# The seams of the two MLPs rebuilt: output projection in groups of 2 and 6 tiles, another order of the up tiles and of the operand loads, and the page sums moved

## The chip, the cores and the metric

One core of a Trainium2 chip runs the whole program. The metric is the device time of one execution in microseconds (us), lower is better. The kernel before takes 2758.23 us, the median of three runs (2755.21 to 2761.97). The names of the engines are those of the profile: PE is TensorE with its weight loads as PEld, DVE is VectorE, ACT is ScalarE, POOL is GpSimd, and SP is SyncE, which here issues nearly all DMAs.

## The reference

One step of a decoder with two layers, on 1088 tokens (1024 of a prompt and 64 of eight samples), model width 1024, hidden width 4096. Layer 0 mixes with a diagonal state-space model (S5) and a gated unit (GLU), layer 1 with a forgetting attention over a paged cache; each also attends to a small memory, and each ends with an output projection, an RMS norm and a squared-ReLU MLP:

```
def rmsnorm(x, g):
    y = x32 * lax.rsqrt(jnp.mean(x32 * x32, axis=-1, keepdims=True) + RMS_EPS)
    return (y * g.astype(jnp.float32)).astype(x.dtype)

def sqrelu_mlp(x, w_up, w_down):
    h = jax.nn.relu(x @ w_up)
    return (h * h) @ w_down
```

The attention of layer 1 also needs, per head, running sums of the log-forget values of the cached rows (the page sums): they are gathered through the page table, summed along the past, and the total is subtracted.

## The kernel before

Activations stand with the model width on the partitions and the tokens along the free dimension. The tokens form four chunks of 272 columns (`CH`); two chunks together are a half (`g`), so the two halves hold chunks 0 and 1, and 2 and 3.

Every fp32 operand is split into a high part, rounded by ACT, and a low part, the rest, subtracted by DVE (`split`, L213, L220 and L221); three matmuls then make one product (`mm3`). The big products of the MLP go through a scheme with seven sub-products instead of eight (`seven`, L390): an operand matrix of 2 by 2 blocks is turned into seven combinations (`operands`, L340, for the activations, with the subtractions L350, L351, L354 and L357; `weight_ops`, L363, for the weights, with four additions on POOL, L379 to L385), and all seven are split.

The stretch this document is about runs once in each layer:

1. The mixer ends. In layer 0 that is the GLU, with the attention to memory (`mem_attn`, L596) beside it. Then POOL issues 16 indirect DMAs that gather the page rows (L1220).
2. The output projection (`out_proj`, L316, over `dense`, L239) has eight weight tiles of 128 columns in two groups of four. For each group the four chunks are gone through in order, each tile of a chunk being 24 matmuls, and DVE adds the result to the residual (L323). Between the groups the page sums are worked out on DVE in layer 0 (L1225 to L1229).
3. With the second group of tiles a chunk is complete and `mlp_norm` (L419) starts: squares on ACT (L257), their sums on DVE (L259, L260), a matmul with ones for the sum over partitions, the scale (L271 to L274), eight multiplications of DVE by the scale and the gain (L432), and then the operands of the up projection; all that needs one chunk alone for chunks 0 and 2, and what combines both chunks of a half for chunks 1 and 3.
4. The up projection (`mlp`, L448) runs over 16 weight tiles `j`, each of 168 matmuls in seven products (12 matmuls for one product and one half), with the first tile done half by half. Its results are squared (L487 to L489), made into the seven operands of the down projection (`to_hidden`, L460), and stored in DRAM as `hops` (operand i, block b = j // 2); those of tiles 14 and 15 are stored plainly as `hcnv`.
5. The down projection (L524) runs over blocks 0 to 6 of the hidden width with seven operands each, loaded from `hops` by SP in pieces of 1088 KB (L514) into eleven places taken in turn (`hplace`), and block 7 is done plainly from `hcnv`. Each block is four passes of seven products of 12 matmuls.

The program is written in text order and then reordered, engine by engine, by a scheduler that simulates a timeline; buffers are rings and carved phases, and whoever writes a buffer waits for its last readers. Each engine then goes through its own list in order, SP's list of DMA issues too.

## Time and profile before

| what | value |
|---|---|
| median of 3 runs | 2758.23 us (2755.21 to 2761.97) |
| the profiled execution | 2760.94 us, of which its span on the core 2759.2 us |
| PE busy | 2575.1 us, 93% of the span, 20345 matmuls |
| DVE busy | 2023.4 us, 73% |
| POOL busy, ACT busy | 1249.9 us and 1239.9 us, 45% each |
| DMA | 561.64 MB, 204 GB/s over the span |
| mean granted clock of PE | 0.97 |

Busy time is the time in which an engine has an instruction in work. A stretch in which PE is less than fully busy is read with the count of matmuls in it: the same number at the pace of a full stretch would need less time, and the difference is what the stretch loses. Places in the trace are given in microseconds from the start of the span; layer 0's output projection begins near 405 and layer 1's near 1932.

### The profile page before, as it was taken

Reading aid. Unit: us, or ns where it says so; the run is one execution under the profiler, and the core shown is the slowest. Engines: PE = TensorE matmul, PEld = TensorE weight load, DVE = VectorE, ACT = ScalarE, POOL = GpSimd, SP = SyncE. Lnnn points to the kernel's source line nnn. Section 1 sums busy time; section 2 is a strip of 40 time slices with the busy share of each in tenths; the row PEclk is TensorE's granted clock in tenths of the full one; section 3 lists DMA queues with packets and bytes.
Section 4 is the critical chain, followed back from the end, with each engine's and each line's share of the span. In section 5 each row is a group of like instructions: output and inputs, shape, how many; then the busy total and the mean of one; then the engine's idle time right before and its main releaser. Section 6 shows DMA issues by size and latency. Waiting matters only on the chain.

```text
span 2759.2 us, 54020 instructions
## 1 busy us (share of the span) xinstructions
PE 2575.1 (93%) x20345; PEld 2404.4 (87%) x20345; DVE 2023.4 (73%) x3421; ACT 1239.9 (45%) x2544; POOL 1249.9 (45%) x1142
## 2 busy tenths in 40 slices
PE   5887898799998999999999999999879999899998
PEld 5877798799997999999889867777879999799997
DVE  8898655999985777784323278885499999577776
ACT  5433542566663222244322377773256666422224
POOL 4577411332231699842311455551033233169984
PEclk8999899899998999999999999999989999999999
DMA  6445332265668566543476899984226556866741
GB/s 200 109 110 165 105 122 83 82 248 229 234 241 314 208 258 266 198 157 108 147 261 218 265 303 312 305 296 159 96 88 249 230 236 238 306 238 242 280 170 65
DMA packets 242282, 561.64 MB, mean 204 GB/s; under 512 B 54053, under 2 KB 129382, under 8 KB 224614
## 3 DMA queue, kind: packets, MB, share of 16 engines
q1 hardware_dynamic: 212646, 548.50, 55.5%
q10 hardware_dynamic: 28864, 8.92, 1.4%
q8 instruction: 160, 2.62, 0.4%
q0 software_dynamic: 512, 0.79, 0.1%
q14 instruction: 100, 0.82, 0.1%
HBM read 386.19 MB, written 171.93 MB: 202 GB/s over the span
## 4 chain that ended last, share of the span: by engine, by line
PE 56%; DVE 18%; POOL 9%; DMA 8%; issue 4%; ACT 4%; another core or an unknown queue 1%; SPq 0%; POOLq 0%; ACTq 0%; DVEq 0%
PE banks L208 54%; DVE rounded L221 5%; POOL plain L539 4%; DMA hops<-plain 2%; DVE plain L221 2%; DMA rounded<-hops 2%; PE banks L1558 1%; POOL plain L547 1%; ACT rounded L220 1%; POOL plain L381 1%; POOL plain L379 1%; POOL plain L380 1%; ACT plain L220 1%; POOL plain L385 1%
## 5 line engine op out<-in xcount | busy, mean ns | idle before, releaser
L208 PE MATMUL banks<-rounded 128*128 128x272 f32 (+4 forms) x11552 | 1626.2, 296 | 97.6 <-ACT rounded L220 27.7
L208 PEld LDWEIGHTS banks<-rounded 128*128 128x128 f32 x11552 | 1521.3, 192 | 148.4 <-issue 32.2
L220 ACT ACTIVATE rounded<-plain 128x512 fp32r<-128x512 f32 (+5 forms) x575 | 384.3, 679 | 641.5 <-PE banks L208 473.2
L221 DVE TENSOR_TENSOR rounded<-plain,rounded 128x512 fp32r<-128x512 f32 (+4 forms) x520 | 490.8, 954 | 107.4 <-ACT rounded L220 103.3
L208 PE MATMUL banks<-mlp,rounded 128*128 128x272 f32 x3840 | 526.2, 292 | 18.0 <-DVE plain L536 5.4
L208 PEld LDWEIGHTS banks<-mlp,rounded 128*128 128x128 f32 x3840 | 502.1, 191 | 24.2 <-DVE rounded L221 8.0
L379 POOL TENSOR_TENSOR plain<-plain 128x512 f32<-128x512 f32 x60 | 98.5, 1642 | 709.2 <-DVE rounded L221 709.2
L539 POOL TENSOR_TENSOR plain<-plain,flex 128x544 f32<-128x544 f32 x192 | 292.0, 1531 | 42.0 <-DVE plain L538 39.3
L221 DVE TENSOR_TENSOR plain<-plain 128x544 fp32r<-128x544 f32 x212 | 209.8, 1006 | 28.0 <-ACT plain L220 21.9
L220 ACT ACTIVATE plain<-plain 128x544 fp32r<-128x544 f32 x212 | 136.6, 653 | 187.9 <-DMA hops<-plain 103.6
L538 DVE TENSOR_TENSOR plain<-banks,plain 128x544 f32<-128x544 f32 x192 | 137.7, 718 | 57.7 <-PE banks L208 54.9
L385 POOL TENSOR_TENSOR plain<-plain 128x512 f32<-128x512 f32 x60 | 101.1, 1685 | 65.6 <-DVE rounded L221 65.0
L208 PE MATMUL banks<-layer 128*32 128x256 f32 (+3 forms) x1152 | 110.7, 368 | 5.4 <-ACT layer L1381 2.1
L208 PE MATMUL banks<-flexr,rounded 128*128 128x272 f32 x768 | 107.4, 288 | 1.9 <-DVE flexr L221 1.9
L221 POOL TENSOR_TENSOR rounded<-plain,rounded 64x512 fp32r<-64x512 f32 (+2 forms) x55 | 77.4, 1414 | 67.4 <-ACT rounded L220 61.9
L221 POOL TENSOR_TENSOR rounded<-flex,rounded 128x544 fp32r<-128x544 f32 (+7 forms) x100 | 66.7, 675 | 87.7 <-ACT rounded L220 75.0
L208 PEld LDWEIGHTS banks<-flexr,rounded 128*128 128x128 f32 x768 | 100.6, 188 | 2.3 <-DVE flexr L221 2.3
L381 POOL TENSOR_TENSOR plain<-plain 128x512 f32<-128x512 f32 x60 | 101.1, 1685 | 3.0
L220 ACT ACTIVATE rounded<-banks 128x512 fp32r<-128x512 f32 (+2 forms) x136 | 75.0, 559 | 51.8 <-PE banks L1558 28.8
L221 DVE TENSOR_TENSOR rounded<-banks,rounded 128x512 fp32r<-128x512 f32 (+2 forms) x136 | 86.0, 637 | 15.1 <-ACT rounded L220 13.2
L487 DVE TENSOR_TENSOR plain<-banks,plain 128x544 f32<-128x544 f32 (+1 forms) x136 | 92.6, 681 | 4.7 <-PE banks L208 4.4
L380 POOL TENSOR_TENSOR plain<-plain 128x512 f32<-128x512 f32 x60 | 93.2, 1553 | 4.7
(359 smaller groups left out, 3135.2 us busy)
## 6 DMA issues: line engine op xcount, KB each, us to landing
hops<-plain SPq DMA_DIRECT2D x196, 544.0 KB
rounded<-hops SPq DMA_DIRECT2D x66, 1088.0 KB
plain<-in_cache_kT SPq DMA_DIRECT2D x128, 384.0 KB
layer<-in_cache_v SPq DMA_DIRECT2D x128, 384.0 KB
mlp<-hops SPq DMA_DIRECT2D x32, 1088.0 KB
plain<-in_w_up SPq DMA_DIRECT2D x32, 1024.0 KB
plain<-in_w_down SPq DMA_DIRECT2D x28, 1024.0 KB
plain<-in_xT SPq DMA_DIRECT2D x8, 1088.0 KB
```

The source lines that it names most:

```text
L208: PE.matmul(out, a, b, start=first, stop=last)
L220: S.activation(H, src, AF.Copy)
L221: e.tensor_tensor(L, src, H.bitcast(F32), op=ALU.subtract)
L379: G.tensor_tensor(a22, a21, a22, op=ALU.add)
L380: G.tensor_tensor(a21, a11, a21, op=ALU.subtract)
L381: G.tensor_tensor(a11, a22, a11, op=ALU.subtract)
L385: G.tensor_tensor(a12, a12, a11, op=ALU.subtract)
L487: V.tensor_tensor(x, ps, u, op=ALU.add)
L538: V.tensor_tensor(h, ps, h, op=ALU.add)
L539: G.tensor_tensor(h, h, u, op=ALU.add)
L547: G.tensor_tensor(hc, hc, hr[:, m, :], op=ALU.add)
L1558: PE.transpose(tb[:, k, 128 * i:128 * i + 128], p[i][:, 2 * c + k, :], ident)
```

## The change

It has five parts.

- **Output projection.** The groups are now 2 tiles and 6 tiles. The split weights of tiles 6 and 7 lie in two of the four `Pq` places of the MLP. The step between the groups is gone.
- **Norm.** Except for the last chunk, the sums of squares are made by POOL, and the eight multiplications of DVE become one multiplication by the scale over 128x2176 elements on DVE and eight multiplications by the gain on ACT; the low parts of operands 2 and 6 are split by POOL. Operand 6 of the first half is put off until the norm of the last chunk.
- **Up tiles.** The order is 14, 0, 1, ..., 13, 15, and tile 14's weights have their low parts split by POOL.
- **Up to down.** The weights and all seven operand loads of block 0 are asked for behind the products of tile 15 and ahead of that tile's own stores; the places and their order are new, the loads are issued in a chain, each behind the one before, and the load of the residual stands behind the operands of its block.
- **Page sums.** The 16 indirect DMAs and the sums stand in the text of the GLU loop (before chunk 1 and before chunk 3) and use raw weight buffers (`wf[2:4]`). The scheduler puts the DMAs ahead of that, among POOL's last S5 units.

The core of the diff:

```diff
-    def out_proj(ys, w, hs, done, between=None):
-        for g in range(2):
-            if g and between:
-                between()
-
+    def out_proj(ys, w, hs, done):
+
+        Pq[:] = phase_mlp()
+        more = [Pq[i].sub(WT * j, WT).at([128, 8, 128], F32R) for i in (2, 3) for j in range(2)]
...
+        for g, n in ((0, 2), (2, 6)):
...
-            dense([w[4 * g + i] for i in range(4)], ys, ev, done=(lambda c: done(hs[c], c)) if g else None)
+            dense([(m, w[m]) for m in range(g, g + n)], ys, ev, load, done=(lambda c: done(hs[c], c)) if g else None)
...
         w = CH[c][1]
-        s1 = rms_sums(h, w)
+        last = c == NC - 1
+        s1 = rms_sums(h, w, V if last else G)
         SY.dma_start(out=hmid[c], in_=h)
...
         def rest():
             rs = rms_scale(s1, w)
-            for k in range(8):
-                V.scalar_tensor_tensor(x[:, k, :], h[:, k, :], gains[:, gi, k:k + 1], rs,
-                                       op0=ALU.mult, op1=ALU.mult)
+            if last:
+                for k in range(8):
+                    V.scalar_tensor_tensor(x[:, k, :], h[:, k, :], gains[:, gi, k:k + 1], rs,
+                                           op0=ALU.mult, op1=ALU.mult)
+            else:
+                V.tensor_tensor(x, h, rs[:, None, :].broadcast_to([128, 8, w]), op=ALU.mult)
+                for k in range(8):
+                    S.mul(x[:, k, :], x[:, k, :], gains[:, gi, k:k + 1])
...
+                    split(o[:, 0], o[:, 1], t, G if i in (2, 6) and not last else V)
...
+            if c % 2 == 0:
+                operands(*b, extra, put_of(g), (0, 2))
+            elif not last:
+                operands(*b, extra, put_of(g), (1,))
+                held.append(lambda: operands(*b, extra, put_of(g), (6,)))
+            else:
+                held.pop()()
+                operands(*b, extra, put_of(g), (1, 6))
...
+        hplace = [setB[2], setB[3], setB[0], setC[2], setB[1], *Pq, setC[3], setC[1]]
...
+        def load_on(to, src):
+            with after(loads[-1]) if loads else nullcontext():
+                loads.append(SY.dma_start(out=to, in_=src))
+
+        def next_operands(b):
+
+            t = [hring([128, 2, 2, 2 * CN], F32R) for _ in range(7)]
+            r = [t[i] for i in (0, 5, 1, 6, 2, 3, 4)] if b == 0 else t
+            for i in range(7):
+                load_on(r[i].bitcast(F32), hops[i][b])
+            return r
...
+        jorder = (14, *range(14), 15)
+        W = up_weights(14, G)
+        for n, j in enumerate(jorder):
...
             if j < 15:
-                W = up_weights(j + 1)
-            to_hidden(j, q, tmps(sh))
+                W = up_weights(jorder[n + 1])
+            else:
+                W = down_weights(0, 0)
+                ops = next_operands(0)
+            to_hidden(j, q)
...
+        if c == 1:
+            past_rows()
+        if c == 3:
+            past_sums()
```

Where instructions move, at three places. First SP's list at the step from up to down of layer 0. `hops0` to `hops6` are the stored operands, `rounded`, `mlp1` to `mlp3` the places that they are loaded into, `hcnv` the plain stores of the last tiles. Before:

```order
L514 DMA mlp1_4125<-hops6_76 128x2176
L514 DMA rounded_65<-hops1_71 128x2176
L514 DMA mlp2_4126<-hops0_70 128x2176
L514 DMA rounded_65<-hops2_72 128x2176
L514 DMA mlp3_4127<-hops1_71 128x2176
L514 DMA rounded_65<-hops3_73 128x2176
L477 DMA hcnv_77<-plain_64 128x2x272
L514 DMA rounded_65<-hops4_74 128x2176
L477 DMA hcnv_77<-plain_64 128x2x272
L514 DMA rounded_65<-hops2_72 128x2176
L514 DMA rounded_65<-hops3_73 128x2176
L529 DMA rounded_65<-hmid0_78 128x2176
```

And now:

```order
L515 DMA rounded_65<-hops4_74 128x2176
L515 DMA rounded_65<-hops5_75 128x2176
L515 DMA rounded_65<-hops6_76 128x2176
L490 DMA hops5_75<-plain_64 128x1088
L490 DMA hops4_74<-plain_64 128x1088
L515 DMA mlp2_3588<-hops0_70 128x2176
L515 DMA mlp3_3589<-hops1_71 128x2176
L490 DMA hops6_76<-plain_64 128x1088
L515 DMA rounded_65<-hops2_72 128x2176
L515 DMA rounded_65<-hops3_73 128x2176
L376 DMA plain_64<-in_w_down 128x2x1024
L501 DMA hcnv_77<-plain_64 128x2x272 x8
```

Before, loads of block 0 (operands 0 to 4) and of block 1 (operands 0 to 3) alternate, with `hcnv` stores among them. Now the loads of block 0 stand together, then four loads of block 1, and the eight `hcnv` stores of tile 15 follow those and a load of down weights.

Second, POOL's list from the memory attention to the first up tile in layer 0. L699 before and L734 now are a step of the memory attention; L260 and L261 now are the sums of the norm, L222 a low part of a split, L379 and L386 (with their neighbours) the additions for up weights. Before:

```order
L699 TENSOR_SCALAR glu0_2469<-glu0_2469,plain_64 128x256 x4
L1197 TENSOR_TENSOR plain_64<-rounded_65 128x272 x6
L699 TENSOR_SCALAR glu0_2469<-glu0_2469,plain_64 128x256 x10
L1220 DMA logf0_3563<-in_logf_rows,plain_64 96x128 x16
L379 TENSOR_TENSOR plain_64<-plain_64 128x512
L380 TENSOR_TENSOR plain_64<-plain_64 128x512
L381 TENSOR_TENSOR plain_64<-plain_64 128x512
L385 TENSOR_TENSOR plain_64<-plain_64 128x512
```

And now:

```order
L734 TENSOR_SCALAR glu0_2469<-glu0_2469,plain_64 128x256 x10
L260 TENSOR_TENSOR flex0_69<-flex0_69 128x544 x3
L261 TENSOR_TENSOR flex0_69<-flex0_69 128x272
L260 TENSOR_TENSOR flex0_69<-flex0_69 128x544 x2
L222 TENSOR_TENSOR rounded_65<-plain_64,rounded_65 128x1088
L260 TENSOR_TENSOR flex0_69<-flex0_69 128x544
L261 TENSOR_TENSOR flex0_69<-flex0_69 128x272
L260 TENSOR_TENSOR flex0_69<-flex0_69 128x544 x3
L261 TENSOR_TENSOR flex0_69<-flex0_69 128x272
L222 TENSOR_TENSOR rounded_65<-plain_64,rounded_65 128x512
L386 TENSOR_TENSOR plain_64<-plain_64 128x512
L387 TENSOR_TENSOR plain_64<-plain_64 128x512
```

The gather of the page rows is gone from here, and the sums of three chunks with low parts among them have come in.

Third, POOL's list in the last S5 units of layer 0. L1096, L1103, L1105 and L1106 (now L1131, L1138, L1140 and L1141) are the steps of one unit. Before:

```order
L1103 TENSOR_TENSOR flex0_69<-plain_64 64x2x128 x2
L1105 TENSOR_TENSOR prep0_150<-plain_64 128x2
L1106 TENSOR_TENSOR prep0_150<-plain_64 128x2
L1088 MEMSET plain_64 128x4
L1096 TENSOR_TENSOR plain_64<-plain_64 128x512
L1103 TENSOR_TENSOR flex0_69<-plain_64 64x2x128 x2
L1105 TENSOR_TENSOR prep0_150<-plain_64 128x2
L1106 TENSOR_TENSOR prep0_150<-plain_64 128x2
L1096 TENSOR_TENSOR plain_64<-plain_64 128x512
L1103 TENSOR_TENSOR flex0_69<-plain_64 64x2x128 x2
```

And now:

```order
L1227 DMA plain_64<-in_logf_rows,plain_64 96x128 x2
L1138 TENSOR_TENSOR flex0_69<-plain_64 64x2x128 x2
L1140 TENSOR_TENSOR prep0_150<-plain_64 128x2
L1141 TENSOR_TENSOR prep0_150<-plain_64 128x2
L1123 MEMSET plain_64 128x4
L1227 DMA plain_64<-in_logf_rows,plain_64 96x128 x2
L1080 TENSOR_TENSOR plain_64<-plain_64,prep0_150 128x256
L1131 TENSOR_TENSOR plain_64<-plain_64 128x512
L1227 DMA plain_64<-in_logf_rows,plain_64 96x128 x4
L1131 TENSOR_TENSOR plain_64<-plain_64 128x512
L1138 TENSOR_TENSOR flex0_69<-plain_64 64x2x128 x2
L1140 TENSOR_TENSOR prep0_150<-plain_64 128x2
```

The indirect DMAs, 16 in all, now stand among the steps of the last units, in groups of up to four, and four of the L1138 steps behind them also wait for their landing.

## Rows read from the trace of the kernel before

**Rows 1.** The engines' busy time on the page, with the share of the span and the number of instructions.

```profile
PE 2575.1 (93%) x20345; PEld 2404.4 (87%) x20345; DVE 2023.4 (73%) x3421; ACT 1239.9 (45%) x2544; POOL 1249.9 (45%) x1142
```

**Rows 2.** The table of windows: the window and its length, then busy time of PE, PEld, DVE, ACT and POOL with the instructions that began in it, the granted clock, the DMA share and GB/s. Output projection begins, norm to up, up loop, up to down and down loop of layer 0; then norm to up, up loop and up to down of layer 1.

```profile
405.00:430.00 25.00, 13.93 (x94) 12.41 (x94) 2.62 (x5) 1.34 (x3) 15.23 (x16) 0.80 0.18 46
488.00:549.00 61.00, 46.91 (x280) 43.82 (x279) 59.46 (x85) 31.23 (x51) 17.98 (x9) 0.83 0.18 63
549.00:813.00 264.00, 263.66 (x2092) 263.22 (x2090) 241.49 (x312) 166.74 (x285) 84.75 (x52) 1.00 0.61 237
860.00:896.00 36.00, 22.43 (x122) 20.78 (x122) 9.78 (x15) 4.95 (x9) 4.16 (x3) 0.76 0.87 342
945.00:1140.00 195.00, 191.33 (x1502) 188.40 (x1502) 153.92 (x188) 48.25 (x80) 187.38 (x138) 1.00 0.63 242
2005.00:2066.00 61.00, 46.57 (x287) 42.43 (x286) 60.13 (x86) 31.27 (x52) 18.83 (x9) 0.86 0.18 66
2066.00:2360.00 294.00, 294.00 (x2337) 294.00 (x2336) 269.58 (x348) 189.39 (x322) 92.08 (x56) 1.00 0.61 236
2376.00:2409.00 33.00, 20.03 (x120) 18.86 (x121) 9.50 (x14) 4.75 (x8) 4.15 (x3) 0.84 0.92 364
```

**Rows 3.** The chain of waits where layer 1's output projection begins: start, us, what held it.

```profile
1932.50 7.19 DMA plain<-hscr
```

**Rows 4.** PE's timeline at the step from up to down in layer 0, with the idle time before and its releaser in brackets.

```profile
862.38 1.89 PE L208 MATMUL banks<-rounded 128*128 128x272 f32 x12 [2.27 <-DMA rounded<-hops]
867.65 3.06 PE L208 MATMUL banks<-rounded 128*128 128x272 f32 x12 [3.38 <-DMA rounded<-hops]
872.93 2.16 PE L208 MATMUL banks<-rounded 128*128 128x272 f32 x12 [2.22 <-DMA rounded<-hops]
...
882.84 1.77 PE L208 MATMUL banks<-rounded 128*128 128x272 f32 x12 [1.45 <-DVE flex L412]
885.72 1.77 PE L208 MATMUL banks<-rounded 128*128 128x272 f32 x12 [1.10 <-ACT flex L402]
889.83 2.08 PE L208 MATMUL banks<-mlp,rounded 128*128 128x272 f32 x12 [2.34 <-DVE plain L536]
```

**Rows 5.** SP's timeline at the same place; a long time is a wait in which the issue stands.

```profile
862.31 3.38 SPq L514 DMA_DIRECT2D rounded<-hops  x2
...
872.85 12.08 SPq L477 DMA_DIRECT2D hcnv<-plain  x6
```

**Rows 6.** The chain of waits from 400 to 432, in order of time: start, us, what held the chain.

```profile
411.38 1.84 another core or an unknown queue
413.68 15.12 another core or an unknown queue
428.82 0.45 DVE plain L323
429.32 2.86 PE banks L208 x11
```

**Rows 7.** POOL's timeline in the same stretch, the first two and the last of the 16 indirect DMAs: start, us, and in brackets the idle time before.

```profile
405.83 1.14 POOL L1220 DMA_INDIRECT logf<-in_logf_rows,plain  x1 [8.64 <-ACT flex L713]
407.28 0.92 POOL L1220 DMA_INDIRECT logf<-in_logf_rows,plain  x1 [0.31 <-issue]
...
424.72 0.92 POOL L1220 DMA_INDIRECT logf<-in_logf_rows,plain  x1 [0.30 <-issue]
```

**Rows 8.** DVE's timeline between norm and up projection in layer 0.

```profile
488.13 1.28 DVE L354 TENSOR_TENSOR plain<-plain 128x1088 f32<-128x1088 f32 x1
...
492.87 2.38 DVE L357 TENSOR_TENSOR plain<-plain,flex 128x1088 f32<-128x1088 f32 x1
...
502.23 0.43 DVE L323 TENSOR_TENSOR plain<-banks,plain 128x272 f32<-128x272 f32 x1
...
517.42 3.39 DVE L432 SCALAR_TENSOR_TENSOR plain<-plain,flex 128x272 f32<-128x272 f32 x8
```

**Rows 9.** POOL's timeline in the same stretch.

```profile
485.89 6.50 POOL L379 TENSOR_TENSOR plain<-plain 128x512 f32<-128x512 f32 x1 [60.26 <-DVE rounded L221]
492.47 1.63 POOL L380 TENSOR_TENSOR plain<-plain 128x512 f32<-128x512 f32 x1
...
521.50 1.28 POOL L379 TENSOR_TENSOR plain<-plain 128x512 f32<-128x512 f32 x1 [22.84 <-DVE rounded L221]
```

**Rows 10.** Two groups of section 5 of the page, of POOL: times run, busy us and mean ns of one.

```profile
L379 POOL TENSOR_TENSOR plain<-plain 128x512 f32<-128x512 f32 x60 | 98.5, 1642 | 709.2 <-DVE rounded L221 709.2
L539 POOL TENSOR_TENSOR plain<-plain,flex 128x544 f32<-128x544 f32 x192 | 292.0, 1531 | 42.0 <-DVE plain L538 39.3
```

**Rows 11.** POOL's timeline in the last five S5 units of layer 0: the step of the first, the third and the last of them that waits for DVE, with the idle time before it.

```profile
227.12 1.80 POOL L1096 TENSOR_TENSOR plain<-plain 128x512 f32<-128x512 f32 x1 [2.79 <-DVE plain L1094]
...
244.49 1.79 POOL L1096 TENSOR_TENSOR plain<-plain 128x512 f32<-128x512 f32 x1 [3.12 <-DVE plain L1094]
...
258.92 1.79 POOL L1096 TENSOR_TENSOR plain<-plain 128x512 f32<-128x512 f32 x1 [3.02 <-DVE plain L1094]
```

**Rows 12.** DVE's timeline between the two groups of tiles in layer 0: the second scan and the two subtractions of the page sums.

```profile
439.72 2.34 DVE L1225 TENSOR_TENSOR_SCAN logf<-plain,logf 96x1024 f32<-96x1024 f32 x1
...
443.51 1.41 DVE L1229 TENSOR_SCALAR logf<-logf,plain 96x1024 f32<-96x1024 f32 x2
```

More of the change, by code (lines that the diff above doesn't have):

```diff
@@ L340, in yoco_step, with operands @@
     turn = {"w": 0, "bank": 0}
-    xplace, Pq = [None, None], []
-    def operands(b11, b12, b21, b22, extra, put, which=(0, 1, 2)):
+    xplace, Pq, held = [None, None], [], []
+    def operands(b11, b12, b21, b22, extra, put, which=(0, 1, 2, 6)):
         if 0 in which:
@@ L374, in put @@
         def put(i, x):
-            split(r[i][:, 0], r[i][:, 1], x)
+            split(r[i][:, 0], r[i][:, 1], x, e if i else V)
         put(0, a11)
@@ L440, in rest, with put_of, put @@
             extra = (nt0, setA[1])[g].at([128, 4, w]) if c % 2 else None
-            def put(i, t):
-                o = xop(i, g)
-                split(o[:, 0], o[:, 1], t)
-            operands(x0[:, 0:4], x[:, 0:4], x0[:, 4:8], x[:, 4:8], extra, put, (1,) if c % 2 else (0, 2))
+            b = x0[:, 0:4], x[:, 0:4], x0[:, 4:8], x[:, 4:8]
+            def put_of(g):
+                def put(i, t):
+                    o = xop(i, g)
+                    split(o[:, 0], o[:, 1], t, G if i in (2, 6) and not last else V)
+                return put
@@ L468, in to_hidden @@
             if b < 7:
-                operands(q[0][0], q[0][1], q[1][0], q[1][1], extra, put)
+                operands(q[0][0], q[0][1], q[1][0], q[1][1], tmps(sh), put)
                 return
@@ L477, in to_hidden, with down_weights @@
                         SY.dma_start(out=to[:, i, :, n], in_=t[:, i].bitcast(F32))
-        W = up_weights(0)
-        for j in range(16):
-            tmp = [tmps(sh) for _ in range(3)]
-            q = [[tmps(sh) for _ in range(2)] for _ in range(2)]
-            for gs in (slice(0, 1), slice(1, 2)) if j == 0 else (slice(0, 2),):
+        def down_weights(b, d):
+            return weight_ops((I["w_down"][l, b, 2 * d:2 * d + 2].rearrange("i p k f -> p i k f"), [2, 4, 256]),
+                              lambda r: tuple(r[:, :, k:4:2, 128 * m:128 * m + 128] for m in range(2) for k in range(2)),
+                              [2, 2, 128])
+        hplace = [setB[2], setB[3], setB[0], setC[2], setB[1], *Pq, setC[3], setC[1]]
+        hring = Ring(hplace)
+        residual = setC[0]
+        loads = []
+        def load_on(to, src):
[10 more added lines that the diff above has]
+        for n, j in enumerate(jorder):
+            take = tmps if n else first
+            tmp = [take(sh) for _ in range(3)]
+            q = [[take(sh) for _ in range(2)] for _ in range(2)]
+            for gs in (slice(0, 1), slice(1, 2)) if n == 0 else (slice(0, 2),):
                 def out(m, n, ps, u):
@@ L504, in mlp @@
         tmps = Ring([small.sub(544 * i, 544) for i in range(6)])
[L505 to L524 removed]
+        for b in range(7):
+            if b:
+                ops = next_operands(b)
+            if 0 < b < 5:
+                hr = residual.at([128, 8, CN])
+                load_on(hr, hmid[b - 1])
             for d in range(2):
[L526 to L529 removed]
+                if b + d:
+                    W = down_weights(b, d)
                 for e in range(2):
```

100 lines of the change are left out of this document (43 added, 57 removed).

## The prediction

> **What bounds the kernel now.** I read the busy times first: PE works through 93% of the span, so a change can only gain where PE stands idle, and must not add idle time elsewhere [rows 1]. The table of windows then tells where that is. In layer 0's up loop PE is busy 263.66 of 264 us with 2092 matmuls, 0.126 us for each; every other window is measured against that pace [rows 2]. Where the output projection begins, 94 matmuls need 11.8 of 25.0 us, so 13.2 are lost. From norm to up, 280 and 287 matmuls need 35.3 and 36.2 of 61: 25.7 and 24.8 lost. From up to down, 122 and 120 need 15.4 of 36 and 15.1 of 33: 20.6 and 17.9 lost. Last, the chain of waits has 7.19 us for a residual load in layer 1 [rows 3]. Together 109.4 us, the most that this change could give. The granted clock in the disturbed windows is 0.76 to 0.86, in the up loops 1.00 [rows 2]; part of the loss may be clock, which comes back only if PE stays fed.
>
> What ends each wait I read from the chain and the timelines. From up to down PE waits three times for a load of an operand, and its products begin 5.27 and 5.28 us apart (862.38, 867.65, 872.93) [rows 4]: two loads of 1088 KB pass for each product, one of block 0 and one of block 1, as the order of SP has it. Then six issues of stores hold SP for 12.08 us [rows 5] while PE waits 1.45, 1.10 and 2.34 us for DVE and ACT [rows 4]. From norm to up DVE is the bound, busy 59.46 of 61 us [rows 2]. At the start of the output projection the chain holds 15.12 us that no engine of the profile explains, beside the 16 indirect DMAs on POOL [rows 6, 7].
>
> **Start of the output projection, layer 0.** The indirect DMAs leave this place, and with them, I take it, the unexplained wait. But group 1 is now 2 tiles of 4 chunks and 24 matmuls, 192 instead of 384, so PE has less to do beside the last steps of the memory attention: by the order 61 matmuls fewer, 7.7 us. The chain of those steps gets shorter when matmuls no longer stand between its own; I count two thirds of the filler as such (none and all are the bounds), so 2.6 us stay as idle. The load of the last memory result adds some 0.8. Of 13.2 lost, 3.4 stay: gain 9.8, between 0 and 13.2.
>
> **The same, layer 1.** 96 matmuls of filler, 12.1 us, are gone ahead of the residual wait; by the same two thirds 4.0 us are lost. In return 24 matmuls, 3.0 us, come to stand inside that wait of 7.19. Net −1.0, between −12 and +3.
>
> **Norm to up.** Before, all four norms crowd behind the last chunks, since group 2 gave a chunk only 4 tiles of 3.0 us. Now a chunk has 6 tiles, 144 matmuls, 18.1 us, and the order shows norm and operands of chunks 0 to 2 beside the tiles of the next chunks. Left behind the last tile is the last chunk's own chain. Before, it went from 502.23 to the end of the eight multiplications at 520.81 (517.42 + 3.39), 18.6 us [rows 8]; with the norm before it out of the way I count 14.4 from the order: 9.0 for its own steps and 5.4 for what stands between them on DVE. Behind it DVE has eight operations of 128x1088 at 1.28 (row 488.13), a few small ones, and splits for the first down products: operand 6 of the second half comes 28.1 us after the last tile, tile 14 ends some 3 later, 31. By the order 156 of that tile's 168 matmuls stand behind the last tile of the projection, 19.6 us. Loss 11.4.
>
> That sum has each DVE operation at its undisturbed time. The rows say more: the same operation of 128x1088 takes 1.28 us, and 2.38 when POOL is at work (492.87, beside POOL's L380 from 492.47), while POOL's L379 of 128x512 takes 1.28 alone and 6.50 beside a DVE that never pauses [rows 8, 9]. So work moved from DVE to POOL isn't free for DVE: each overlap costs it about 1.1 us, and POOL needs 1.53 us for 128x544 and 1.64 for 128x512 on average [rows 10]. Of POOL's new work some three operations fall into the last chain with no slack to absorb them: +3.0. Loss 14.4, so the gain is 25.7 − 14.4 = 11.3 and 24.8 − 14.4 = 10.4: 21.7, between 0 and 27.7 for both.
>
> The Trainium skill, "SBUF — State Buffer", section "Who interferes with whom", has a rule that speaks against this part: a DVE instruction with two SBUF inputs contends with a GpSimd instruction that reads SBUF, and the one that comes second stands until the other is done. The trace agrees (2.38 for 1.28). If all of POOL's moved work had to be taken out of DVE's time, the gain of this part would be gone; that is the first rival.
>
> **Up to down.** By the order, block 0's seven loads are asked for during tile 15 and stand together; at 2.64 us each (half of 5.27) they take 18.5 us, less than the tile's 168 matmuls, 21.2. The waits for loads go. What is late next: the eight plain stores of tile 15 stand on SP behind four loads of block 1 and one of weights, 5 × 2.64 = 13.2 us. ACT's fourth split of that tile waits for its buffer, which the first stores still read, and behind it on ACT stand the rest of the weight splits and the first copy of the second pass. Loads begin to flow for block 1 near the tile's end, PE has a first pass of 84 matmuls (10.6 us) to work on and 36 more before the banks run out, so about 15 us of cover against a store that lands some 20 to 23 after the tile: 5 to 8 us of stall, and I take 8.0. Gain 20.6 − 8.0 = 12.6 and 17.9 − 8.0 = 9.9: 22.5, between −10 (a stall of 24 in each) and 32.
>
> **S5 units.** The indirect DMAs now stand on POOL among the S5 units. The sixteen start 1.26 us apart ((424.72 − 405.83) / 15 [rows 7]), 20.1 us. In the last five units POOL is idle for about 2.9 us each before its first step [rows 11], 14.7 in all (all five added up). The rest, 5.4, I charge in full, though the stage behind has slack, since the landing is waited for as well: −5.4, between 0 and −20.1. DVE's page sums, two scans of 2.34 and two subtractions of 1.41 together, 6.1 us [rows 12], go from a place with slack to another where I take it that DVE is not the bound: 0, to −6.1. The down loop, where POOL is busy 187.38 of 195 us [rows 2], is not touched.
>
> **Sum.** 9.8 − 1.0 + 21.7 + 22.5 − 5.4 = 47.6. The profiled execution took 2760.9, so 2713.3; it lies 2.7 above the median of the runs: 2710.6, say 2711.
>
> **Rivals.** First, POOL and DVE stand in each other's way and the norm still ends as late as before: for it speaks the 6.50 us of rows 9, against it that the three earlier chunks have 18 us each. Without the 21.7: 2733. Chance 0.13.
>
> Second, the stores behind the block 1 loads hold up the start of the down loop for 16 us instead of 8, in both layers: for it the 12.08 us of rows 5, against it that PE has two passes of loaded data. 2711 + 16 = 2727. Chance 0.13.
>
> Third, the better case: no stall by the stores beyond 3 us (+10), no lock on the path (+6), the units' slack takes the indirect DMAs (+5): 2690. Chance 0.10.
>
> Fourth, slower: the wait of 15.12 us is the landing of indirect DMAs, not their issue [rows 6]. Four S5 steps on POOL now wait for a landing; each such wait would stop the unit chain, which PE, DVE and POOL go through in turn. At 15 us each that is 60, less the 3 of slack in each: 2711 + 48 = 2759, with the tails' fillers at their bound (−11) 2770. It makes the kernel slower from about 15 us per place, and eats a quarter of the gain at 6. Against it: 1.26 us of spacing in rows 7 shows no backpressure. Chance 0.07.
>
> Fifth, the change doesn't do what it says: the scheduler's order meets other waits at each seam and most of the loss stays, 2755. Chance 0.04.
>
> **How the numbers follow.** My forecast has 0.53, with 2697 to 2724 as its own range. To leave out no more than 2 in 10 I go from 2684 (the third rival and a little) to 2746 (the first two together, 2749, nearly). What can be told from no change is 0.3%, 8.3 us. Slower by more than that only in the fourth rival with company: 0.06. Within: the fifth, part of the fourth: 0.06. Faster: 0.88.
>
> **What would show it.** In the profile after: at the norm, 128x2176 multiplications of DVE under the projection tiles, and PE reaching the second up tile about 31 us after the last projection tile; more than 40 means the first rival. From up to down, no PE wait for operand loads, and one wait behind ACT near the end of the first pass of block 0; its length tells the second rival. In the S5 units POOL's idle time before its first step gone, the stage longer by no more than some 6 us; waits for landing of over 10 us are the fourth. A gain of PE's idle time that the granted clock doesn't follow would make the forecast too low.

## The result and the profile after

The changed kernel takes 2765.49 us against 2759.61 before, a ratio of 1.0017 (95% interval 1.0010 to 1.0024): 0.2% slower, less than the 0.3% that I called no change. The forecast was 2711 with a range down to 2684 and up to 2746. One of the changed kernel's 20 runs took 3534.56 us at a granted clock of 0.65 and is not in the ratio. So the change did a great deal, as the order showed, and the sum of it came out at nothing.

To see where, I take the start of the n-th matmul in both traces; the change adds and removes none (20345 in each), so the difference at the same n tells how far one kernel is ahead or behind at that place. The columns are the changed kernel and six of the experiments below, each minus the kernel before, in us.

```
    n  place                         before  after     e1     e2     e3     e4     e5     e9
 1500  S5 units                       244.4   -0.3   -2.7   -1.7   -1.6   -0.2   -2.1   -3.0
 2500  end of the GLU                 394.2    8.7    8.5   10.3    8.7   -0.1    9.9    7.2
 2750  output projection, layer 0     440.2   -0.6   -1.1    0.9   -0.1   -8.3    0.6   -1.4
 3500  up loop, layer 0               560.9   -3.2   -3.7   -1.9   -6.2  -10.9   -9.9  -11.1
 5700  end of the up loop             838.8   -3.3   -3.8   -2.2   -6.3  -11.3  -10.8  -11.9
 6000  down loop                      897.5   -4.2   -1.5  -14.4   -8.6  -13.2  -12.8  -23.1
 7500  last blocks of the down loop  1091.0    0.2   -1.6   -9.2   -3.7   -8.6   -7.5  -18.5
 9000  layer 1 begins                1288.5    0.0   -1.6   -9.4   -4.0    4.0   -8.0  -20.4
14750  output projection, layer 1    1989.8    5.8    0.4   -4.3   -0.5    4.9   -6.7  -21.8
15250  up loop, layer 1              2078.1    2.7   -1.8   -6.7   -5.9    2.6  -14.1  -29.1
17500  end of the up loop            2361.4    2.7   -1.8   -6.7   -5.9    2.6  -14.1  -29.1
17750  down loop                     2411.2    2.7    1.8  -15.9   -6.2    2.4  -13.5  -37.7
20340  end                           2744.8    8.0    1.8  -10.9   -0.8    7.7   -9.2  -32.8
```

Each column is one trace. Those of e1, e2, e3, e5 and e9 lie at −1.6 to −3.0 at n = 1500, which their edits do not reach, and the changed kernel's at −0.3; so a step of under 3 us in one column alone proves little.

Read down the column "after", the steps are: S5 +9.0 (8.7 + 0.3), start of the projection −9.3, norm to up −2.6 (−0.6 to −3.2), up to down −0.9, down loop +4.4, layer 1 up to its projection +5.6, norm to up −3.1, up to down 0, down loop +5.3. Only the second is what I had counted.

PE is busy 5 us less over the span than in [rows 1], DVE 60 less and POOL 60 more, as the page has it:

```profile
PE 2569.8 (93%) x20345; PEld 2401.5 (87%) x20345; DVE 1963.9 (71%) x3337; ACT 1253.5 (45%) x2592; POOL 1310.3 (47%) x1184
```

The windows at the seams, with the columns of [rows 2], first the start of the projection and norm to up and up to down of layer 0, then the same two seams of layer 1:

```profile
409.00:434.00 25.00, 25.00 (x189) 24.46 (x189) 8.99 (x15) 6.74 (x10) 2.72 (x2) 0.93 0.31 99
480.00:541.00 61.00, 44.19 (x302) 41.21 (x301) 52.44 (x61) 30.01 (x53) 39.57 (x18) 0.92 0.14 52
863.00:899.00 36.00, 22.59 (x135) 21.54 (x135) 17.70 (x23) 7.57 (x12) 5.48 (x4) 0.76 0.71 272
2005.00:2066.00 61.00, 45.80 (x311) 43.73 (x310) 52.48 (x64) 30.13 (x55) 38.34 (x17) 0.92 0.16 56
2379.00:2412.00 33.00, 19.43 (x122) 18.37 (x121) 12.06 (x18) 7.74 (x15) 3.88 (x4) 0.74 0.90 356
```

The first window held 94 matmuls before and now 189, with PE busy throughout. Norm to up holds 302 instead of 280 in 61 us, 22 × 0.126 = 2.8 us better. Up to down of layer 1 holds 122 instead of 120: nothing. At norm to up PE is busy for less of the window than before, 44.19 us for 46.91, so it stands idle 16.8 us instead of 14.1; the gain is in the matmuls, which took less time each at a granted clock of 0.92 instead of 0.83. Note the DVE and POOL columns there: DVE issues fewer instructions (61 for 85) and is still busy 52.44 us, while POOL went from 17.98 to 39.57.

**Norm to up.** DVE's timeline of the changed kernel in that seam, with durations (second column) to hold against [rows 8]:

```profile
488.26 1.18 DVE L272 TENSOR_TENSOR flex<-flex 128x272 f32<-128x272 f32 x1
489.36 1.81 DVE L260 TENSOR_TENSOR flex<-flex 128x544 f32<-128x544 f32 x1
...
503.36 2.96 DVE L222 TENSOR_TENSOR rounded<-plain,rounded 128x1088 fp32r<-128x1088 f32 x1 [3.59 <-ACT rounded L221]
...
508.32 2.42 DVE L261 TENSOR_TENSOR flex<-flex 128x272 f32<-128x272 f32 x1
...
520.47 1.29 DVE L356 TENSOR_TENSOR plain<-plain 128x1088 f32<-128x1088 f32 x1
...
527.68 1.29 DVE L363 TENSOR_TENSOR plain<-plain 128x1088 f32<-128x1088 f32 x1
```

And POOL's, where the first two run beside DVE's operations of 2.96 and 2.42 us, and the last beside DVE's row from 520.47 on:

```profile
502.63 2.54 POOL L222 TENSOR_TENSOR mlp<-plain,mlp 128x1088 fp32r<-128x1088 f32 x1
505.12 5.32 POOL L222 TENSOR_TENSOR rounded<-plain,rounded 128x512 fp32r<-128x512 f32 x2
...
520.69 9.41 POOL L392 TENSOR_TENSOR plain<-plain 128x512 f32<-128x512 f32 x1 [5.16 <-DVE rounded L222]
```

An addition over 128x272 that takes 0.43 us took 2.42 on DVE; one of 128x512 that takes 1.28 alone took 9.41 on POOL, from 520.69 to 530.10, just while DVE ran its row of operand steps without a pause (520.47 to 528.97). Behind that addition ACT's list held a weight split and behind the split an operand's, and PE waited 5.07 us for ACT. First ACT's line, then PE's:

```profile
530.14 0.63 ACT L221 ACTIVATE rounded<-plain 128x512 fp32r<-128x512 f32 x1 [4.83 <-POOL plain L392]
...
520.61 1.83 PE L209 MATMUL banks<-rounded 128*128 128x272 f32 x10 [3.85 <-DVE rounded L222]
...
534.72 0.82 PE L209 MATMUL banks<-mlp,rounded 128*128 128x272 f32 x2 [5.07 <-ACT rounded L221]
```

**Up to down.** PE's timeline, against [rows 4]:

```profile
866.09 2.83 PE L209 MATMUL banks<-rounded 128*128 128x272 f32 x12 [2.61 <-DMA rounded<-hops]
870.11 3.09 PE L209 MATMUL banks<-rounded 128*128 128x272 f32 x12 [1.20 <-DVE flex L419]
874.21 1.77 PE L209 MATMUL banks<-mlp,rounded 128*128 128x272 f32 x12 [1.00 <-ACT flex L409]
884.58 5.80 PE L209 MATMUL banks<-rounded 128*128 128x272 f32 x24 [8.60 <-DVE plain L571]
```

Of the three waits for loads one is left, as the order had it. In their place stands one of 8.60 us for DVE's L571, which adds results of the first pass of the down projection into `H5` (in layer 1 it is 8.19 us). `H5` lies over `setA`, where the buffers of the `hcnv` stores are, and the chain names what L571 waited for:

```profile
851.91 15.37 DMA hops<-plain
867.28 0.02 issue
867.30 0.67 ACT plain L221
867.98 15.72 DMA hcnv<-plain
883.71 0.03 issue
883.76 0.04 issue
883.80 0.73 DVE plain L571
```

A store that is issued at 867.98 lands at 883.70. It stands on SP behind four loads of block 1 and one of weights, 5 × 2.64 = 13.2 us. ACT's split that the prediction had in mind waits for the same stores, 8.8 us, and starts at 885.39, 1.6 us behind DVE's L571.

**Down loop.** POOL, which is busy nearly as long as PE there [rows 2], waits in layer 0 for the residual load; before the change the same table has no such row:

```profile
POOL plain L582 <- DMA rounded<-hmid: 5.6, 3, 2.3
```

**S5.** The chain in the last units and behind them (first the gather, then the page sums' scan and subtractions on DVE, then the load of S5's results into the GLU):

```profile
255.07 1.03 POOL plain L1227
...
273.48 2.75 DVE plain L1233
...
285.34 1.33 DVE plain L1237 x2
...
290.13 7.20 DMA plain<-yscr
```

**Start of the projection, layer 1.** The residual wait of [rows 3] is as long as before:

```profile
1926.90 7.26 DMA plain<-hscr
```

### The profile page after: what moved, and what is told of

The parts are those of the page before. It is cut to its first block, busy times and chain, and to the rows that moved or that the text cites. A ratio compares the mean times of both kernels' runs of the same rounds, so it can differ in the third digit from the quotient of the medians.

```text
span 2766.5 us, 54068 instructions
## 1 busy us (share of the span) xinstructions
PE 2569.8 (93%) x20345; PEld 2401.5 (87%) x20345; DVE 1963.9 (71%) x3337; ACT 1253.5 (45%) x2592; POOL 1310.3 (47%) x1184
## 4 chain that ended last, share of the span: by engine, by line
PE 44%; DVE 22%; DMA 13%; POOL 9%; issue 6%; ACT 5%; SPq 1%; POOLq 0%; ACTq 0%; DVEq 0%
PE banks L209 42%; DMA hops<-plain 7%; DVE rounded L222 6%; POOL plain L574 4%; DVE plain L222 3%; POOL plain L392 1%; ACT plain L221 1%; PE banks L1599 1%; DMA rounded<-hmid 1%; DVE plain L536 1%; POOL plain L582 1%; DMA hcnv<-plain 1%; ACT rounded L221 1%; POOL plain L388 1%; POOL plain L386 1%
## 5 line engine op out<-in xcount | busy, mean ns | idle before, releaser
L209 PE MATMUL banks<-rounded 128*128 128x272 f32 (+3 forms) x11168 | 1561.3, 296 | 108.6 <-ACT rounded L221 28.2
L209 PEld LDWEIGHTS banks<-rounded 128*128 128x128 f32 x11168 | 1465.6, 192 | 156.3 <-ACT rounded L221 31.9
L222 DVE TENSOR_TENSOR rounded<-plain,rounded 128x512 fp32r<-128x512 f32 (+4 forms) x500 | 509.0, 1022 | 119.8 <-ACT rounded L221 114.1
L386 POOL TENSOR_TENSOR plain<-plain 128x512 f32<-128x512 f32 x60 | 91.5, 1525 | 488.9 <-DVE rounded L222 488.7
L222 DVE TENSOR_TENSOR plain<-plain 128x544 fp32r<-128x544 f32 x212 | 165.0, 788 | 87.3 <-ACT plain L221 84.1
L392 POOL TENSOR_TENSOR plain<-plain 128x512 f32<-128x512 f32 x60 | 118.2, 1970 | 88.4 <-DVE rounded L222 87.9
L222 POOL TENSOR_TENSOR rounded<-plain,rounded 64x512 fp32r<-64x512 f32 (+4 forms) x71 | 112.0, 1586 | 76.9 <-ACT rounded L221 69.5
L537 ACT ACTIVATE plain<-plain 128x544 f32<-128x544 f32 (+1 forms) x136 | 85.3, 628 | 79.2 <-DVE plain L536 78.8
L222 POOL TENSOR_TENSOR rounded<-flex,rounded 128x544 fp32r<-128x544 f32 (+7 forms) x100 | 67.3, 681 | 86.7 <-ACT rounded L221 74.0
L222 DVE TENSOR_TENSOR rounded<-banks,rounded 128x512 fp32r<-128x512 f32 (+2 forms) x136 | 85.9, 636 | 14.1 <-ACT rounded L221 12.2
L260 POOL TENSOR_TENSOR flex<-flex 128x544 f32<-128x544 f32 x18 | 27.6, 1533 | 138.9 <-ACT flex L258 90.9
```

The source lines that it names most:

```text
L209: PE.matmul(out, a, b, start=first, stop=last)
L222: e.tensor_tensor(L, src, H.bitcast(F32), op=ALU.subtract)
L386: G.tensor_tensor(a22, a21, a22, op=ALU.add)
L392: G.tensor_tensor(a12, a12, a11, op=ALU.subtract)
L537: S.activation(x, x, AF.Relu)
```

## The experiments

Times are medians; "below" and "above" are against the changed kernel's 2765.49 where nothing else is said, and the ratio is that to the kernel before. The kernel before was run beside each group of experiments (e1 to e4, e5 to e8, e9 to e11, e12), at medians of 2755.92 to 2758.81; across groups the ratios compare better than the times.

**e1: the residual load of the down loop issued as before.**

```diff
-            if 0 < b < 5:
-                hr = residual.at([128, 8, CN])
-                load_on(hr, hmid[b - 1])
             for d in range(2):
                 if b + d:
                     W = down_weights(b, d)
+                if d == 0 and 0 < b < 5:
+                    hr = residual.at([128, 8, CN])
+                    SY.dma_start(out=hr, in_=hmid[b - 1])
```

> Edit: the residual load of the down loop is issued as before the change (inside the block, behind its first down weights, no longer chained behind the block's operands); all else as changed. The changed kernel's matmuls of both down loops ran 4.2 and 5.3 us later against the kernel before than they had at the loops' start, and POOL there waited three times (1.60, 2.32, 1.71 us in layer 0) for this load. Theory (the chained residual load stops POOL, which bounds the down loop): both losses go, 9.5 us, time about 2756, POOL's waits for the load gone. Rival (POOL is late because of the work that the new order hands it, the load only shows it): under 2 us, time 2764 to 2766.

2761.95 us, ratio 1.0008 (0.9998 to 1.0017). Both down loops lose nothing now (−1.5 to −1.6, and 1.8 to 1.8 in the table), and POOL's waits for the load are gone, so the theory holds for the loops. But the seams ahead of them lose 2.3 us (−3.8 to −1.5) and 3.6 (−1.8 to 1.8) where the changed kernel gained 0.9 and lost nothing; PE's wait for DVE's L419 there grew from 1.20 to 3.58. So the time fell by about a third of the 9.5 us that I expected.

**e2: the plain stores of tile 15 ahead of block 1's loads.**

```diff
-                        SY.dma_start(out=to[:, i, :, n], in_=t[:, i].bitcast(F32))
+                        stores.append(SY.dma_start(out=to[:, i, :, n], in_=t[:, i].bitcast(F32)))
...
+            if b == 1:
+                loads.append(stores[-1])
             for i in range(7):
                 load_on(r[i].bitcast(F32), hops[i][b])
```

> Edit: the first operand load of block 1 is chained behind the last plain store of tile 15, so that the stores stand ahead of the four loads and not behind them. Theory (up to down gained nothing since the stores land late behind those loads, and the down results wait to overwrite the buffer that the stores read; PE waited 8.60 us for the first such result in layer 0): that wait falls below 2 us, some 7 us gained in each layer, time about 2751. Rival (the stores are slow in themselves, 12.08 us for six before and 15.7 now in the chain): the wait stays above 5 us and the time is 2760 to 2766.

2744.98 us, ratio 0.9942 (0.9926 to 0.9959). PE's waits in the seam of layer 0 are these, and the one for L571 is not among them:

```profile
867.24 2.77 PE L209 MATMUL banks<-rounded 128*128 128x272 f32 x12 [1.81 <-DMA rounded<-hops]
871.38 3.09 PE L209 MATMUL banks<-rounded 128*128 128x272 f32 x12 [1.37 <-DVE flex L419]
875.47 1.77 PE L209 MATMUL banks<-mlp,rounded 128*128 128x272 f32 x12 [1.00 <-ACT flex L409]
```

The seams give 12.2 us (−2.2 to −14.4) and 9.2 (−6.7 to −15.9), where the changed kernel had 0.9 and 0. The theory holds, and the gain is larger than the 7 us in each layer that it expected; of the waits for the stores themselves, 0.6 us of ACT in layer 0 is left. The rival, that the stores are slow in themselves, falls. That 12.2 and 9.2 are near the 12.6 and 9.9 of the prediction is luck: the prediction had 8.0 us of stall by the stores in them, and e2 has none.

**e3: one weight addition of the second up tile on DVE.** `weight_ops` takes an engine for its last addition, V for the second tile of the up order, POOL elsewhere.

```diff
-        G.tensor_tensor(a12, a12, a11, op=ALU.subtract)
+        last.tensor_tensor(a12, a12, a11, op=ALU.subtract)
```

> Edit: for the second up tile of each layer alone, the last of the four weight additions goes from POOL to DVE. Theory (this addition, which took 9.41 us on POOL while DVE ran without a pause, held ACT's list, ACT held the last operand's split, and PE waited 5.07 us): PE's wait goes, 4 to 5 us gained per layer, time about 2756; the extra DVE operation costs 0.7. Rival (DVE's own chain of operands would have ended as late anyway): under 1.5 us per layer, time 2763 to 2767.

2759.62 us, ratio 1.0005 (0.9995 to 1.0015). Norm to up gives 6.1 and 5.4 us instead of 2.6 and 3.1: 3.5 and 2.3 more, and PE's wait of 5.07 fell to 1.58. That is less than the 4 to 5 us expected, but this addition is one part of the loss; the seam is still far from the 11.3 and 10.4 forecast.

**e4: the page work in layer 1.** The calls leave the GLU loop and stand between two groups of the query projection:

```diff
     dense([I["w_in1"][i] for i in range(4)], xn, ev_q1, gained(1), each=mem_tick)
+    past_rows()
+    past_sums()
```

> Edit: the page gather and sums go from the GLU's text to layer 1, between the query projection's two groups of tiles, so that neither the S5 units nor the output projection has them. Theory (the gather costs 8.9 us in the S5 stage by POOL's and DVE's lists, and the 9.3 us gained at the output projection come from its absence there): the S5 stage ends 8 to 9 us earlier, the output projection keeps its gain, time about 2757, or less by nothing, more by up to 5 if layer 1 has to wait. Rival (the S5 stage is longer by another cause, such as the order of its other work): the S5 stage keeps its 8.9, time 2765 or more.

2768.82 us, ratio 1.0035 (1.0022 to 1.0047). The S5 stage loses nothing (−0.1 at n = 2500) and the projection's start still gains 8.2 (−8.3): so the page work (the gather and the sums, moved together) is what the S5 stage paid for, and its absence is what the projection gained. But where it went, 12.9 us are lost (−8.9 at n = 8500, 4.0 at 9000), and the 2757 expected was missed.

**e5: POOL's new work at the norm back on DVE.**

```diff
-        s1 = rms_sums(h, w, V if last else G)
+        s1 = rms_sums(h, w, V)
...
-                    split(o[:, 0], o[:, 1], t, G if i in (2, 6) and not last else V)
+                    split(o[:, 0], o[:, 1], t, V)
...
-        W = up_weights(14, G)
+        W = up_weights(14, V)
```

> Edit: the work that the change gave to POOL at the norm goes back to DVE (sums of squares of all chunks, the low parts of operands 2 and 6, the low parts of tile 14's weights); all else as changed. In the changed kernel DVE's operations with two SBUF inputs ran far above their undisturbed time there (0.44 us ones took 1.2 to 2.4, a 1.28 us one 2.96). Theory (POOL and DVE stand in each other's way, so the move gave DVE little): the seam from norm to up loses at most 1 us more than in the changed kernel or gains up to 4 in each layer, time 2757 to 2768. Rival (the move pays as I counted, DVE's added work of some 14 us per layer lands on the path): 5 us or more lost per layer, time 2776 or more.

2749.64 us, ratio 0.9965 (0.9951 to 0.9979): 16 us below (14 by the ratios), more than even the theory had allowed, and the rival falls. Norm to up now gives 10.5 us in layer 0 (0.6 to −9.9) and 7.4 in layer 1, 12.2 more than in the changed kernel; most of the rest lies between the down loop of layer 0 and the projection of layer 1, which the edit does not touch. DVE has more to do and is sooner through. Its operations that stood beside POOL's norm work now take their undisturbed time; beside POOL's weight additions, which stay, some are still stretched (L272 takes 1.48 us at 510.23). DVE in e5, the two steps that took 2.96 and 2.42:

```profile
502.45 1.29 DVE L222 TENSOR_TENSOR rounded<-plain,rounded 128x1088 fp32r<-128x1088 f32 x1 [1.29 <-ACT rounded L221]
...
506.55 0.43 DVE L261 TENSOR_TENSOR flex<-flex 128x272 f32<-128x272 f32 x1
```

And the addition that took 9.41 on POOL, now done ahead of DVE's operand steps:

```profile
512.91 1.26 POOL L392 TENSOR_TENSOR plain<-plain 128x512 f32<-128x512 f32 x1
```

**e6: the page work beside the plain block of layer 0's down projection.** The calls leave the GLU loop and are handed to `mlp`:

```diff
         W = [wall(I["w_down"][l, 7, i], [128, 4, 256]) for i in range(4)]
+        if beside:
+            beside()
...
-    mlp(0, hs, mlp0_done, add_square)
+    mlp(0, hs, mlp0_done, add_square, lambda: (past_rows(), past_sums()))
```

> Edit: the page gather and sums stand beside the last, plain block of layer 0's down projection, in raw weight buffers that are idle there, and not in the GLU's text. With the gather among layer 1's first products (e4) the S5 stage's loss went, but 13 us were lost there. Theory (the gather costs what it queues on POOL and DVE ahead of work that PE waits for, and nothing beside a stretch where PE has its operands): the S5 loss of 8.9 goes, no new loss, time about 2757. Rival (indirect DMAs hold PE up wherever they run): 8 to 13 us lost beside the plain block, time 2765 to 2770.

2768.71 us, ratio 1.0043 (1.0029 to 1.0057). While the gather ran, from 1177 to 1201, PE waited 2.7 us in all (0.17, 0.43 and 2.13, the last for DVE): indirect DMAs don't hold PE up by themselves, and the rival falls in that form, though the time is the one that it named. But 13.4 us were lost by the time that layer 1's first products were through (−9.8 at n = 8000, 3.6 at 9000), so the theory's "no new loss" fell too. The page sums' scan and subtractions stand on DVE's list there, and the next weights' loads wait for the raw buffers; which of these weighs more I did not part.

**e7 and e8: three and four repairs together.** Their diffs are those of e2, e3 and e6, and of e1 besides for e8.

> Edit: three repairs together: the stores of tile 15 ahead of block 1's loads (e2), the second up tile's last weight addition on DVE (e3), the page work beside the plain block (e6). Theory (the three losses are independent): the gains of e2 (20.5) and e3 (5.9) and 9 for the pages add up, 35 below the changed kernel, time about 2730. Rival (a gain in one seam is given back in the next): 2740 or more.

2746.90 us, ratio 0.9957 (0.9941 to 0.9974). The repairs show in their seams (at the places of the table, 5.4 us from norm to up and 10.6 from up to down in layer 0), but where the page work stands now 16.2 us are lost (−19.3 at n = 8000, −3.1 at 9000), and the 2730 expected was missed.

> Edit: as e7, and the residual load of the down loop issued inside the block as before the change (e1). Theory (the chained residual load costs some 4 us in each down loop, and e1 gave part of that back only since its up to down seam got worse behind the late stores, which e2 removes): 7 to 9 us below e7, about 2722. Rival (e1's worse seam comes from the new order of loads itself): within 3 us of e7.

2747.04 us, ratio 0.9956 (0.9939 to 0.9972): no gain over e7, the rival's side. The down loops lose nothing now, but up to down gives 2.6 and 2.9 us less than in e7, and the attention stage takes the rest.

**e9: e2 and e5 together**, with both diffs.

> Edit: e2 and e5 together: the stores of tile 15 ahead of block 1's loads, and the norm's moved work back on DVE. Theory (the two losses stand in different seams and add up): 20 and 16 below the changed kernel, about 2730, clearly faster than both kernels. Rival (what one seam gains the next gives back): 2738 or more.

2730.10 us, ratio 0.9904 (0.9888 to 0.9921): the theory. By the ratios e2 and e5 are 21 and 14 us below the changed kernel, together 35, and e9 is 31 below; that the median is 2730 as expected is in part luck. In the seams the two add up: norm to up gives 9.7 and 7.3 us (10.5 and 7.4 in e5), up to down 11.2 and 8.6 (12.2 and 9.2 in e2). The window of norm to up holds 357 matmuls in 61 us where the kernel before had 280 and the changed one 302, and POOL's busy time there is down to 15.85:

```profile
480.00:541.00 61.00, 50.02 (x357) 47.99 (x357) 55.49 (x78) 35.08 (x62) 15.85 (x11) 0.92 0.27 90
```

**e10: e9 with e1's diff.**

> Edit: e9 with the residual load of the down loop issued inside the block as before the change (e1). Theory (the loss of the down loops, 4 to 5 us each, goes, and 2 to 3 us per layer are lost from up to down, as e8 against e7 showed): 2 to 4 us below e9. Rival (the later stage, whose loads fill the DMA engines, takes it back, as in e8): within 2 us of e9.

2730.39 us, ratio 0.9900 (0.9884 to 0.9917): the rival. What the loops gain (4.6 us in layer 0's), the seam ahead of them and the attention stage take back.

**e11: e9 with the sums of squares on POOL again.** Against e9:

```diff
-        s1 = rms_sums(h, w, V)
+        s1 = rms_sums(h, w, V if last else G)
```

> Edit: e9 with the sums of squares of the first three chunks on POOL again, as in the changed kernel; the low parts (operands 2 and 6, tile 14's weights) stay on DVE. Theory (what costs is POOL working beside DVE behind the last chunk's start; the sums of chunks 0 to 2 run earlier, beside projection tiles): within 3 us of e9. Rival (any operation of POOL with two inputs from SBUF costs DVE on its path, the sums as much as the low parts): 6 to 14 us above e9.

2737.86 us, ratio 0.9928 (0.9912 to 0.9945): 7.8 above e9, and norm to up gives 3.2 and 3.3 us less. My theory fell: the sums, though they run early, cost as well. DVE's operations beside them are stretched too. The same step of DVE in e9 and in e11, and the sum on POOL that runs beside the latter:

```profile
472.16 1.28 DVE L360 TENSOR_TENSOR plain<-plain 128x1088 f32<-128x1088 f32 x1
...
473.16 2.46 DVE L360 TENSOR_TENSOR plain<-plain 128x1088 f32<-128x1088 f32 x1
...
472.55 1.92 POOL L260 TENSOR_TENSOR flex<-flex 128x544 f32<-128x544 f32 x1 [8.35 <-ACT flex L258]
```

That the sums are slower on POOL is not the reason: that chunk's are done at 481.36 in e11 and at 482.72 in e9. So it is not only the place behind the last chunk that matters; that it is DVE's lack of slack at either place is my reading, and no run tests it alone.

**e12: e9, with the page sums' stores behind the last load of S5's results.**

```diff
-        SY.dma_start(out=zs, in_=yscr[q].rearrange("(t c) g j -> (c g) t j", c=16))
+        zlast = SY.dma_start(out=zs, in_=yscr[q].rearrange("(t c) g j -> (c g) t j", c=16))
...
-            SY.dma_start(out=fpast[:, 1024 * i:1024 * i + 1024], in_=fp[i])
+            with after(zlast):
+                SY.dma_start(out=fpast[:, 1024 * i:1024 * i + 1024], in_=fp[i])
```

> Edit: e9, and the two stores of the page sums are issued only behind the last load of the S5 results, which stood behind them on SP. In the changed kernel those stores were issued at 286.03 once DVE had finished the page sums, and that load at 290.13; before the change the load was issued at 280.76. Theory (of the 8.9 us that the S5 stage lost, the part behind 262 us, some 6, is SP's list held by the page sums): the load is issued by about 284, 5 to 6 us gained, time about 2725. Rival (the stage ends with DVE's and POOL's own work, which the page sums lengthen, and the load is only the last to show it): under 2 us, time 2728 to 2730.

2727.81 us, ratio 0.9893 (0.9877 to 0.9910), 2.3 us below e9 with intervals that overlap, so nearer to the rival than to the theory's 5 to 6: the load was issued at 287.88, not 284. SP's list was not what held it. The chain of e12 in that stretch shows the page work itself:

```profile
254.64 1.03 POOL plain L1229
...
265.04 1.17 POOL plain L1229
...
266.51 2.76 DMA plain<-in_logf_rows,plain
...
272.94 2.75 DVE plain L1235
...
284.80 1.32 DVE plain L1239 x2
```

1.03 + 1.17 + 2.76 + 2.75 + 1.32 = 9.0 us, two issues, a landing, a scan and the two subtractions, each on the chain ahead of the GLU. That is about what the S5 stage lost (7.9 in e12, from −0.6 at n = 1500 to 7.3 at 2500); since the chain before went other ways, it is a sum that fits, not one that is shown.

## Why the prediction was wrong, step by step

- **Start of the projection, layer 0: right.** Forecast 9.8, found 9.3. The unexplained wait of 15.12 us went with the gather.
- **The same, layer 1: near in size, by two terms that were both wrong.** Forecast −1.0; across the fillers and the residual wait (n = 14250 to 14400) it went from 5.9 to 5.7. I had let 24 matmuls, 3.0 us, stand inside the residual wait; the chain shows 7.26 us of it with PE idle, as before. And of the 4.0 that the missing fillers should have cost, PE's waits there show 1.05 us (0.83 and 0.22). Most of the loss from n = 13750 (2.6) to 14250 stands ahead of the fillers, where PE waits 3.54 us behind a load of projection weights, 1.78 before the change and 1.82 in e9.
- **Norm to up: the failing step is the term "+3.0", three overlaps of 1.1 us.** Forecast 11.3 and 10.4, found 2.6 and 3.1. The first rival came nearly true: 5.7 of the 21.7 us are left. I had the row (2.38 for 1.28), and still counted only overlaps on the last chain. Taking POOL's work out (e5) gave back 7.9 and 4.3 us; the sums alone (e11) cost 3.2 and 3.3. The 6.50 us of [rows 9] told the other half: POOL starves as long as DVE doesn't pause, and what hangs on POOL (here a weight addition, then ACT's list, then PE) waits with it. Without the +3.0 my sum gives 14.3 and 13.4; e5, with that work back on DVE, found 10.5 and 7.4, and whether the difference is this work or the rest of the sum was not tested.
- **Up to down: the failing step is that "8.0 us of stall" was taken for the whole loss that stays.** Forecast 12.6 and 9.9, found 0.9 and 0: the second rival's price of 8 more, and beyond. The wait itself came out near its size, 8.60 and 8.19 us, not the rival's 16. That the stores stand behind block 1's loads I had read from the order; they held ACT's split, as I said, and ahead of it DVE's addition into `H5`, which I had not seen. But with the stores put first (e2) the seam gains 11.3 and 9.2 us over the changed kernel, more than the wait, since PE ran slower behind it (24 matmuls in 5.80 us, in e2 in 3.17). And in e2 some 8.4 and 8.7 of the 20.6 and 17.9 us still stay, which I had put at nothing: in layer 0 the waits of 1.81, 1.37 and 1.00 us, and matmuls at about half pace between them (12 in 2.77 and 3.09 us, at full pace 12 × 0.126 = 1.5).
- **Down loop: I wrote "is not touched".** It lost 4.4 and 5.3. The residual load moved from behind the block's weights into the chain of operand loads, and POOL, which I had named as busy 187 of 195 us, waits for it. A row that says an engine has no slack says that a load it needs may not come later; I used it only for instructions.
- **S5: right in sign, short in size.** Forecast −5.4, found −9.0 (to −12.0 in the other columns that have the page work there). I priced POOL's issue alone; a landing, a scan and the subtractions on DVE lie on the chain too (6.8 of the 9.0 us in e12), where I had put 0 for DVE. The fourth rival (landings of 15 us) fell: the longest wait for a landing there was 3.16 us.

With the two main terms repaired, e9 takes 2730, and its trace ends 32.8 us ahead where I had counted 47.6. Beyond my count were taken 9.5 us in the down loops, 4.8 in the S5 stage, 4.7 at the norms, 2.7 from up to down and 1.2 at the projection of layer 0; 8.1 came back in places where I had counted no gain. From layer 1's beginning to its projection the kernels differ by −1.4 (e9) to 5.8 (the changed one) though the change hardly touches that stretch; that is open, and no run was made for it.

## What to carry to other kernels

Here, moving elementwise work from a busy DVE to an idle POOL was not load balancing: count each such operation against DVE as well, and look at what hangs on POOL while DVE runs without a pause. When loads are pulled forward in a queue, write down who stands behind them, and for stores, who waits to overwrite what they read. And where an engine has no slack, a load that it needs is on its list too.

## What the hardware showed beyond expectation

- The work moved to POOL cost more there than on DVE: e5 has DVE do more and is 14 to 16 us faster, 12.2 of them at the two norms, with operations at 0.43 for 2.42 and 1.29 for 2.96 us. The Trainium skill, "SBUF — State Buffer", section "Who interferes with whom", has the rule, a DVE instruction with two SBUF inputs against a GpSimd instruction that reads SBUF; the trace agrees and adds that one POOL instruction can be put off for a whole row of DVE's: 9.41 us for 1.26.
- A store of 272 KB, issued behind five loads of about 1 MB, took 15.72 us to land, and DVE and PE waited for it; with the stores ahead of four of these loads (e2) 0.6 us of ACT was all that waited.
- The page work, a gather of 16 indirect DMAs with its sums on DVE, cost 9 us in the S5 stage, 8 to 9 where it stood before, and 13 to 16 in either of two other places, although PE was not seen to stop for the issues themselves; in e12's S5 stage issues, a landing and DVE's sums stand on the chain.
